# Layer 1's triangular inverses: diagonal blocks of 16 by row steps, joined to 32 by matrix products

## The chip, the cores and the metric

The kernel runs on one core of a Trainium2 chip. The metric is device time in microseconds, the median of three runs. A profiled execution of the kernel before gives the trace from which all times below come. The engines are named as in the profile: PE (matrix products; PEld is its weight load), DVE (vector engine), ACT (activation engine), POOL (GpSimd) and SP (which issues nearly all DMAs).

## The reference, cut to what matters

The reference is one step of a two-layer decoder for 512 prompt tokens and 8 sample tokens, width 1024, float32. Layer 0 mixes windowed attention and a state-space scan; layer 1 is a gated delta net; each is followed by a SwiGLU block. The change touches one thing only, the solve in layer 1's delta rule:

```python
kb = kc * bc[..., None]
a_mat = jnp.einsum('bhcid,bhcjd->bhcij', kb, kc) * dec_strict + jnp.eye(ch)
rhs = jnp.concatenate([vc * bc[..., None], kb * jnp.exp(gcum)[..., None]], axis=-1)
sol = lax.linalg.triangular_solve(a_mat, rhs, left_side=True, lower=True, unit_diagonal=True)
```

For every chunk of tokens and every one of 16 value heads this is a unit lower triangular system, identity plus a strictly lower part made of the keys' products, their decays and beta. The kernel works with chunks of 128 tokens, so it has 4 chunks x 16 heads = 64 systems of 128 x 128, in two groups g of 32 (8 heads by 4 chunks).

## The kernel before, in words

All large projections are float32 products split into hi + lo parts: three products per weight tile, two token halves, 128 output columns at a time (`lin`, line 299, whose products all come from `mm`, line 268). A tile of 128 output columns is 48 PE instructions. The weights are loaded by SP in groups of 1 MB and split by ACT or DVE (hi) and POOL or DVE (lo) in `WStream.split` (lines 148 to 167).

Layer 1 (`l1`, lines 1206 to 1323) goes in this order of the program:

- `kq(g, 0)` (line 1234): four tiles of keys of group g. Each is projected on PE, scaled and convolved (`conv_tile`, line 518: scaling on DVE at line 274, one tap on ACT, one sum on POOL at line 274, multiply-adds on DVE at line 281), and transposed to tokens (`l1_tokens`, PE line 271).
- `l1_system(g)` (line 1423): builds the 32 systems of a group in `s.A[g]` (tiles X and p7): POOL at lines 1439 and 1441 (recorded at the helper's line 274), ACT exponentials, products of keys on PE, a DVE product with them; four 32 x 32 transposes on DVE (line 1457) write the transposed diagonal blocks of 32 to `xt` in p5.
- `l1_eliminate` (line 1461): the inverses of all diagonal blocks of 32, by 31 row steps j for each group, on all 128 partitions at once. A step is two DVE operations: a product of (31 - j) x (j + 1) elements into a scratch in b4 and its subtraction from the rows below in `T` (p5). Both are `tt` (line 274), so the trace shows them as `b<-p` and `p<-p,b`. The steps of the two groups are written alternately. At the end two 32 x 32 transposes per group (lines 1485 and 1486) give the transposed blocks `up` (p5) and the blocks `tn` (b4).
- `l1_combine(g)` (line 1489): blocks of 64 from those of 32, then 128 from 64, by small products on PE into the PSUM ring "ma" (two buffers, `mx`, line 264), with evictions on ACT and DVE between them. A 32-row round is 32 products; two such rounds, twice, and eight rounds of 8 products of 64 rows, for each group.
- `kq(g, 1)` and `l1_queries(g)` (line 1416) for both groups: four tiles of queries each; then a [128, 32] table of query decays is computed on DVE (`sd`), transposed on PE to rows (line 1409, recorded at line 271 as `mb<-cst,sd`), and written to DRAM.
- `v(0)` and `v(1)` (line 1240): eight tiles of values each.
- the two scans (`l1_scan`, line 1547), issued alternately, each chunk's products needing the inverses `U = s.A[g]`, then the sample tokens, the gate projection and the output projection.

Each engine runs its instructions in one fixed order. That order comes from a planner that walks through the program with estimated costs and due times: of the instructions that are ready by its estimate it takes the one that stands first in the program, `high_priority()` work ahead of it. So `l1_eliminate` is preferred to the queries' and values' work wherever its operands are ready. `hold(...)` keeps a stretch of the program from being planned before a given instruction: `hold_v1` is `e030` in the table of choices (line 84), that is, `v(1)` stays behind step 30 of group 0's elimination. `hold_v0` is `s01` (a step of `l1_system(0)`).

What the elimination before consists of:

```python
for j, g in steps:                       # 31 steps, two groups
    nr = 31 - j
    for c0, c1 in ((0, min(j + 1, cut)), (cut, j + 1)):   # cut = 32: one pass
        ...
            s.tt(t, xt[g][:, j, j + 1:32].unsqueeze(2).to_broadcast([128, nr, nn]),
                 T[g][:, j, c0:c1].unsqueeze(1).to_broadcast([128, nr, nn]), ALU.mult, e)
            o = s.tt(T[g][:, j + 1:32, c0:c1], T[g][:, j + 1:32, c0:c1], t, ALU.subtract, e)
```

The scratch of the elimination lies in b4 at 0 and 1024; the combining uses b4 from 0 (`tn`) and from 2048 (the evicted products `zb`); the scans later use b4 for states and decays.

Of the kernel before, what the change touches and what calls it, by code (L numbers as in the profile page):

```python
# [58 lines left out]
def shape_constants():  # L59
# [24 lines left out]
 'hold_v1': 'e030',  # L84
# [37 lines left out]
def KN(n, v, *others):  # L122
    """The engine, share or order chosen at a place: v unless the table has another of the choices."""
    return KNOBS.get(n, v)
# [4 lines left out]
class WStream:  # L129
    """Weights, in the order of use: loaded in groups, split into hi + lo in units of at most 4 row tiles."""  # L130
# [38 lines left out]
    def tile(s, ap, c0, kts, spread=None, ncol=None, out=None):  # L169
        """Yield (row tile, hi, lo) for the 128 columns from c0 and the row tiles kts; input weights come two tiles a load.  # L170
        out = (buffer, offset) of 1024 floats for each four row tiles, to hold them apart from the ring."""
        if ncol is None:
            g = c0 - c0 % 256
            if s.key != (ap.tensor.name, ap.offset, g):
                s.key, s.raw = (ap.tensor.name, ap.offset, g), s.load(ap, 0, 8, g, 256)
            raw, off = s.raw, c0 - g
        else:
            raw, off = s.load(ap, 0, 8, c0, ncol), 0
        for k0 in range(0, len(kts), 4):
            hi, lo = s.split(raw, kts[k0], 4, off, spread, out and out[k0 // 4])  # L180
            for j in range(4):
                yield kts[k0] + j, hi[:, j], lo[:, j]

    def rows(s, ap, c0, loads):
        """As tile() for a tall matrix; loads are (first row tile, count, unit offsets in their order)."""
        for k0, n, offs in loads:
            raw = s.load(ap, k0, n, c0, 128)
            for o in offs:
                m = min(4, n - o)
                hi, lo = s.split(raw, o, m, 0)  # L190
                for j in range(m):
                    yield k0 + o + j, hi[:, j], lo[:, j]


class Ker:
# [14 lines left out]
    def gen(s, *names):  # L210
        """From here on these buffers hold something else: float32r operands and float32 data never share a tile."""
        for n in names:
            s.big[n] = s.sb.tile([128, BIG[n]], F32, tag=n, name=n, bufs=1)

    def lay(s, name, off=0, n=KD, dt=F32R):
        """Operand (tile, half) -> columns, for n tiles of all tokens."""
        t = s.B(name, off, n, NT, dt=dt)
        return lambda k, h: t[:, k, HALF[h]]

    def layh(s, name, n=KD):  # L220
        """As lay(), the first half of the tokens of every tile before the second."""
        return lambda k, h: s.B(name, 256 * n * h + k * HW[h], HW[h], dt=F32R)
# [63 lines left out]
    def cp(s, e, out, in_):  # L286
        """Copy on ACT, DVE or GpSimd."""
# [10 lines left out]
    # ---- linear layers: weights stationary, 520 token columns moving in two halves  # L298
    def lin(s, w, xh, xl, nkt, halves=(0, 1), ps=None):
        """ps[half] = sum over row tiles of w (yielding (row tile, hi, lo)) of hi'xh + hi'xl + lo'xh."""  # L300
# [7 lines left out]
    def group(s, w, xh, xl, nkt):  # L308
        """Up to four tiles, the first half of the tokens of all before the second half, which may come later."""
# [13 lines left out]
    def lnexp(s, ins):  # L323
        """After ins, one table load for Ln and Exp."""
        with s.tc.issue_after(ins):
            s.nc.scalar.preload_act_table_set("natural_log_exp_and_others")

    def rstd(s, out, ps, n, e=EPS, keep=None, after=None):
        """out = rsqrt(ps / n + e), refined by a Newton step; keep = EPS * (ps / n + e)."""
# [17 lines left out]
    # ---- setup  # L347
# [66 lines left out]
    def add_sq(s, h, x, first, tmp, eng=None):  # L414
        """accT += x^2."""
# [7 lines left out]
    def prenorm(s, n, l, hi, lo, h, upd=None):  # L423
        """hi + lo = x * gain, exactly split."""
# [9 lines left out]
    def token_norm(s, h, keep=None):  # L434
        """s.R2 = per-token rsqrt(mean x^2 + eps), on every partition."""
# [7 lines left out]
    def boundary(s, deferred):  # L443
        """x += mp * rsqrt(mean m^2 + eps), then the next layer's prenorm (n, l, hi, lo): the second half, and the norms."""
# [5 lines left out]
    def residual(s, deferred, h):  # L450
        """One half's update of x, as a function of the feature tile."""
# [17 lines left out]
    def out_proj(s, rows, xh, xl, nkt, mp, n, l, pre, tail=2, final=False):  # L469
        """mp = m * gain, accT + sqs = sum m^2 for the eight tiles of an output projection; the last ones by token halves."""  # L470
# [46 lines left out]
    # ---- causal convolution of one 128-feature tile, then silu  # L517
# [26 lines left out]
    def conv_sample(s, nt, new, old, w, bias, out, tmp):  # L544
        """new [128, nt, 8], old [128, nt, 8, 3], w(j) [128, nt]; out [128, nt, 8] = silu(conv)."""
# [12 lines left out]
    def gate_z(s, ps, zt):  # L558
        """zt = silu(z)."""
# [8 lines left out]
    def softplus(s, out, x, n):  # L568
        """out = max(x, 0) + log1p(exp(-|x|)); log1p(e) = 2 atanh(e / (2 + e)) as a series. Shapes [128, n]."""
# [16 lines left out]
    # ---- layer 0: input projection and mixers in the order of issue  # L586
# [78 lines left out]
    # ---- layer 0: sample convolution state  # L665
# [21 lines left out]
    # ---- layer 0: dt, decays in token layout  # L687
# [53 lines left out]
    # ---- layer 0: SSD over four chunks of 128 tokens, for one group of heads  # L741
# [78 lines left out]
    # ---- layer 0: one SSM step per sample  # L820
# [39 lines left out]
    # ---- layer 0: gate, grouped norm  # L860
# [6 lines left out]
    def l0_norm(s, g, zt, yh, yl):  # L867
        """y * silu(z) (in zt), normalised, to the exactly split yh + yl."""
# [11 lines left out]
    # ---- layer 0: attention of the prompt  # L880
# [25 lines left out]
    def l0_tokens(s, hp):  # L906
        """Keys and values token-major: the caches of the prompt and of the samples, V for the products."""
# [82 lines left out]
    # ---- layer 0: attention of the samples over their cached rows  # L990
# [67 lines left out]
    # ---- SwiGLU  # L1058
# [55 lines left out]
    def cache_shift(s):  # L1114
        """The samples' rolling caches: all rows but the oldest move up by one."""
# [11 lines left out]
    def final_early(s):  # L1127
        """x and the norm's eps of the second half token-major."""
# [27 lines left out]
    def final_first(s):  # L1156
        """The first half's outputs; m of the second half token-major, as far as it is known."""
# [26 lines left out]
    def final_last(s):  # L1184
        """The second half's outputs, token-major: x + m * rsqrt(mean m^2 + eps)."""
# [19 lines left out]
    # ---- layer 1: gated delta net, input projection and mixer in the order of issue  # L1205
    def l1(s):
# [64 lines left out]
        for g in range(2):  # L1271
            marks["c%d" % g] = s.l1_combine(g)
# [10 lines left out]
        with hold("hold_v0", "-", "s01", "s02", "s03", "s12", "s13", "e004", "e010", "e020", "e030", "e110"):  # L1283
# [4 lines left out]
        with hold("hold_v1", "e116", "e104", "e110", "e113", "e119", "e122", "e125", "e128", "e130", "c00", "c01", "c02", "c10", "c11", "e020", "e030"):  # L1288
# [36 lines left out]
    def vo(s, g, h, j):  # L1325
        """Half h of the tokens of v head 8 g + j: V token-major, then the outputs feature-major."""
# [5 lines left out]
    # ---- layer 1: beta, decays in token layout  # L1332
# [41 lines left out]
    # ---- layer 1: keys (w = 0) and queries token-major: sums of squares, keys for the state products  # L1374
# [23 lines left out]
    def log_norm(s, g, w):  # L1398
        """-log(sum of squares + eps) / 2 in place, seen per v head."""
# [6 lines left out]
    def bcast_rows(s, t, tag):  # L1406
        """[tokens, 32] to DRAM as 32 rows of 128 tokens."""
# [14 lines left out]
    # ---- layer 1: the 32 (chunk, v head) systems of one half of the heads, I + strictly lower  # L1422
# [37 lines left out]
    # ---- layer 1: transposed unit-triangular inverses in place of the systems: diagonal blocks of 32 by elimination  # L1460
    def l1_eliminate(s, marks):
        nc = s.nc
        cut = KN("cut", 32, 28, 24, 20, 16)
        xt = [s.B("p5", 1024 * g, 32, 32) for g in range(2)]
        T = [s.B("p5", 2048 + 1024 * g, 32, 32) for g in range(2)]
        for g in range(2):
            nc.gpsimd.memset(T[g], 0.0)
            nc.gpsimd.memset(s.B("p5", 2048 + 1024 * g, 1024)[:, 0:1024:33], 1.0)
        steps = [(j, g) for j in range(31) for g in range(2)]
        if KN("eseq", 0, 1):  # L1470
            steps = [(j, g) for g in range(2) for j in range(31)]
        for j, g in steps:
            nr = 31 - j
            for c0, c1 in ((0, min(j + 1, cut)), (cut, j + 1)):
                nn = c1 - c0
                if nn > 0:
                    t = s.B("b4", 1024 * g + 512 * (c0 > 0), nr, nn)
                    e = nc.gpsimd if c0 else None
                    s.tt(t, xt[g][:, j, j + 1:32].unsqueeze(2).to_broadcast([128, nr, nn]),
                         T[g][:, j, c0:c1].unsqueeze(1).to_broadcast([128, nr, nn]), ALU.mult, e)  # L1480
                    o = s.tt(T[g][:, j + 1:32, c0:c1], T[g][:, j + 1:32, c0:c1], t, ALU.subtract, e)
                    if not c0:
                        marks.setdefault("e%d" % g, []).append(o)
# [4 lines left out]
    # ---- layer 1: the inverses of 64 and 128 rows from those of 32  # L1488
# [57 lines left out]
    # ---- layer 1: delta rule over four chunks of 128 tokens, for one half of the heads  # L1546
# [119 lines left out]
    # ---- layer 1: silu(z) times the normalised outputs, split into hi + lo  # L1666
# [16 lines left out]
    # ---- layer 1: sample convolution state  # L1683
# [25 lines left out]
    # ---- layer 1: one delta-rule step per sample: what the states are not needed for  # L1709
# [42 lines left out]
    # ---- layer 1: one delta-rule step per sample: outputs, then (l1_sample_state) states  # L1752
# [133 lines left out]
```

## Time and profile before

| what | us |
|---|---|
| runs | 1904.42, 1915.31, 1905.85 (median 1905.85) |
| span of the profiled execution, first to last instruction | 1901.6 |
| its own time beside the span | not listed; the span is 4.25 below the median of the runs |
| PE busy in the span | 1746.8 |
| DVE busy in the span | 1190.0 |
| first and last elimination operation | 967.62 to about 1104.7 |
| last product of the combining | about 1144.5 |

A row of the trace by time gives its start, its length, the engine, the line, the operation, output and inputs by the program's names, the shape and a count if rows were merged. A float32 product leaves two PE records. PEclk is the clock that PE was granted, 1.0 being full and 0.5 the only lower value in this trace. A wait is put down to the engine that released it.

### The profile page before, as it was taken

The numbers are of one execution on the slowest core, as the hardware profiler recorded it, in microseconds if no ns is written. First come the engines' busy times: TensorE is split into PE (matmuls) and PEld (weight loads), VectorE is DVE, ScalarE is ACT, GpSimd is POOL, SyncE is SP. The second block draws the span as 40 slices with busy tenths as digits, with TensorE's granted clock in tenths as the row PEclk, the third lists the DMA queues.
The fourth block names the chain that finished last, engine by engine and source line by source line (L and its number), as shares of the span: only waits on it lengthen the run. The fifth ranks groups of instructions, "written<-read, shape, count | busy, mean of one in ns | idle before, by whom it ended". The sixth has DMA issues, their size and how long they took to land.

```text
span 1901.6 us, 36269 instructions
## 1 busy us (share of the span) xinstructions
PE 1746.8 (92%) x14263; PEld 1659.2 (87%) x14263; DVE 1190.0 (63%) x2334; ACT 748.7 (39%) x1828; POOL 876.2 (46%) x768
## 2 busy tenths in 40 slices
PE   8899999898999999988968898989889999999996
PEld 7888777698999999977857787978889899999996
DVE  6898878638323221178899977888954954443125
ACT  5432335555222223355756555544334511111222
POOL 2565756234444433435474554646668411112452
PEclk9999999998999999999988899999989899999998
DMA  7345765453333334453442123257998333432333
GB/s 259 125 130 183 237 202 142 145 182 113 111 111 112 112 106 136 124 177 114 137 139 72 59 65 92 63 156 212 272 290 237 132 135 134 134 133 84 92 92 106
DMA packets 293323, 268.88 MB, mean 141 GB/s; under 512 B 11841, under 2 KB 276742, under 8 KB 291986
## 3 DMA queue, kind: packets, MB, share of 16 engines
q1 hardware_dynamic: 292502, 265.90, 45.5%
q8 instruction: 112, 1.84, 0.4%
q10 hardware_dynamic: 652, 0.68, 0.1%
q14 instruction: 57, 0.47, 0.1%
HBM read 241.01 MB, written 62.04 MB: 159 GB/s over the span
## 4 chain that ended last, share of the span: by engine, by line
PE 56%; DVE 26%; DMA 8%; issue 4%; ACT 4%; POOL 2%; SPq 1%; DVEq 0%; POOLq 0%; ACTq 0%
PE acc L268 48%; DVE p L274 4%; DVE cs L281 4%; PE ma L268 4%; PE mb L268 3%; DVE b L274 2%; DVE sq L281 2%; DMA raw<-in_w_ffn_down_dram 2%; DVE p L281 1%; DVE Hh L281 1%; PE mb L271 1%; DVE cs L274 1%; DMA bm<-csd 1%; POOL cs L274 1%; DVE wlo L165 1%
## 5 line engine op out<-in xcount | busy, mean ns | idle before, releaser
L165 POOL TENSOR_TENSOR wlo<-raw,whi 128x512 fp32r<-128x512 f32 (+3 forms) x373 | 500.8, 1346 | 676.7 <-ACT whi L289 368.1
L268 PE MATMUL acc<-Hl,whi 128*128 128x256 f32 (+1 forms) x2576 | 565.6, 291 | 20.2 <-DVE Hl L281 8.5
L268 PEld LDWEIGHTS acc<-Hl,whi 128*128 128x128 f32 x2576 | 420.5, 193 | 35.4 <-issue 11.3
L289 ACT CAST whi<-raw 128x512 fp32r<-128x512 f32 (+3 forms) x392 | 234.4, 602 | 453.0 <-PE acc L268 388.2
L268 PE MATMUL acc<-Hh,whi 128*128 128x256 f32 (+1 forms) x1824 | 387.0, 287 | 3.5 <-DVE cs L274 2.0
L268 PE MATMUL acc<-Hh,wlo 128*128 128x256 f32 (+1 forms) x1824 | 389.0, 288 | 0.0
L268 PEld LDWEIGHTS acc<-Hh,whi 128*128 128x128 f32 x1824 | 292.5, 191 | 8.2 <-issue 5.1
L268 PEld LDWEIGHTS acc<-Hh,wlo 128*128 128x128 f32 x1824 | 292.8, 191 | 7.5 <-issue 6.7
L268 PE MATMUL acc<-bm,whi 128*128 128x256 f32 (+1 forms) x1136 | 237.1, 290 | 1.4 <-DVE bm L281 1.4
L268 PE MATMUL acc<-p,whi 128*128 128x264 f32 (+1 forms) x1280 | 230.6, 287 | 4.4 <-ACT p L1819 1.6
L290 DVE CAST whi<-raw 128x512 fp32r<-128x512 f32 x131 | 61.1, 467 | 256.7 <-PE acc L268 195.2
L165 DVE TENSOR_TENSOR wlo<-raw,whi 128x512 fp32r<-128x512 f32 (+1 forms) x150 | 117.5, 785 | 142.2 <-ACT whi L289 138.8
L268 PEld LDWEIGHTS acc<-p,whi 128*128 128x128 f32 x1280 | 190.6, 192 | 6.4 <-ACT p L1819 1.9
L268 PEld LDWEIGHTS acc<-bm,whi 128*128 128x128 f32 x1136 | 182.1, 193 | 3.7 <-issue 1.6
L268 PE MATMUL acc<-p,wlo 128*128 128x256 f32 (+1 forms) x704 | 164.4, 288 | 8.7 <-DVE wlo L165 7.0
L268 PE MATMUL acc<-Hl,wlo 128*128 128x256 f32 (+1 forms) x752 | 171.1, 293 | 1.0 <-POOL wlo L165 0.9
L268 PEld LDWEIGHTS acc<-Hl,wlo 128*128 128x128 f32 x752 | 126.4, 195 | 3.2 <-POOL wlo L165 1.6
L268 PEld LDWEIGHTS acc<-p,wlo 128*128 128x128 f32 x704 | 119.6, 192 | 10.1 <-DVE wlo L165 7.9
L281 DVE SCALAR_TENSOR_TENSOR cs<-cs,cw 128x512 f32<-128x512 f32 x100 | 96.4, 966 | 12.7 <-POOL cs L274 8.6
L268 PE MATMUL acc<-X,whi 128*128 128x264 f32 (+1 forms) x512 | 100.4, 291 | 1.7 <-DVE X L274 1.3
L268 PEld LDWEIGHTS acc<-X,whi 128*128 128x128 f32 x512 | 80.4, 195 | 3.2 <-DVE X L274 1.6
L281 DVE SCALAR_TENSOR_TENSOR Hh<-cs,CS,Hh 128x256 f32<-128x256 f32 x64 | 53.1, 894 | 26.5 <-POOL Hh L274 26.2
(465 smaller groups left out, 2932.6 us busy)
## 6 DMA issues: line engine op xcount, KB each, us to landing
raw<-in_w_gdn_in_dram SPq DMA_DIRECT2D x24, 1024.0 KB
raw<-in_w_ffn_gate_dram SPq DMA_DIRECT2D x22, 1024.0 KB
raw<-in_w_ffn_up_dram SPq DMA_DIRECT2D x22, 1024.0 KB
raw<-in_w_ffn_down_dram SPq DMA_DIRECT2D x20, 1024.0 KB
raw<-in_w_hyb_in_dram SPq DMA_DIRECT2D x16, 1024.0 KB
out_sv_dram<-in_cache_attn_v_dram SPq DMA_DIRECT2D x16, 1023.0 KB
out_sk_dram<-in_cache_attn_k_dram SPq DMA_DIRECT2D x16, 1023.0 KB
raw<-in_w_gdn_out_dram SPq DMA_DIRECT2D x10, 1024.0 KB
```

The lines of the kernel that those rows point to most:

```text
L165: eng.tensor_tensor(out=lo[:, :nk, d:d + n], in0=raw[:, :, o:o + n], in1=hi[:, :nk, d:d + n].bitcast(F32), op=ALU.subtract)
L268: s.nc.tensor.matmul(out, lhsT=lhsT, rhs=rhs, start=start, stop=stop, skip_group_check=skip)
L271: s.nc.tensor.transpose(out, in_, s.ident[0:in_.shape[0], 0:in_.shape[0]])
L274: return (eng or s.nc.vector).tensor_tensor(out=out, in0=a, in1=b, op=op).ins
L281: return s.nc.vector.scalar_tensor_tensor(out=out, in0=a, scalar=sc, in1=b, op0=op0, op1=op1).ins
L289: return s.nc.scalar.copy(out, in_).ins
L290: return (s.nc.vector if e == "V" else s.nc.gpsimd).tensor_copy(out, in_).ins
```

## The change

The elimination stops at blocks of 16: 15 steps instead of 31. A step now works on both blocks of 16 of each block of 32 in one operation (a first dimension of 2 with the stride from one diagonal block to the next), so that a step is still two DVE operations. A new function `l1_join(g)` makes the blocks of 32 from those of 16: three rounds of 128 products on PE, each of one block (32 systems y, 4 blocks b of 32 rows), 16 columns wide, with one eviction on ACT and two on DVE, and a clearing of half of a scratch `z` on POOL. It is called ahead of `l1_combine(g)`. The table of choices has `hold_v1` at `e014`, the last step of group 0.

```diff
-        steps = [(j, g) for j in range(31) for g in range(2)]
...
-        for j, g in steps:
-            nr = 31 - j
-            for c0, c1 in ((0, min(j + 1, cut)), (cut, j + 1)):
...
+        def both(t, r, c, dims):
+            t = dap(t)
+            return bass.AP(t.tensor, t.offset + 32 * r + c, [list(t.ap[0]), [16 * 33, 2]] + dims)
...
+        for j in range(15):
+            for g in range(2):
+                nr, nn = 15 - j, j + 1
+                t = s.B("b4", 1024 * g, 2, nr, nn)
+                s.tt(t, both(xt[g], j, j + 1, [[1, nr], [0, nn]]), both(T[g], j, 0, [[0, nr], [1, nn]]), ALU.mult)
+                o = both(T[g], j + 1, 0, [[32, nr], [1, nn]])
+                marks.setdefault("e%d" % g, []).append(s.tt(o, o, t, ALU.subtract))
...
+    def l1_join(s, g):
+        nc = s.nc
+        up, tn, A = s.B("p5", 1024 * g, 32, 32), s.B("b4", 1024 * g, 32, 32), s.A[g]
+        z = s.B("b4", 2048, 32, 32)
+        nc.gpsimd.memset(z[:, :, 0:16], 0.0)
+        blocks = [(y, 32 * b) for y in range(32) for b in range(4)]
+        v = lambda ps: ps.rearrange("p (y c) -> p y c", y=32)
+        ps = s.mx("ma")
+        for y, b in blocks:
+            s.mm(ps[b:b + 32, y * 16:y * 16 + 16], A[b:b + 32, y, b:b + 32], up[b:b + 32, y, 16:32])
+        nc.scalar.copy(z[:, :, 16:32], v(ps))
+        pu = s.mx("ma")
+        for y, b in blocks:
+            s.mm(pu[b:b + 32, y * 16:y * 16 + 16], tn[b:b + 16, y], z[b:b + 16, y, 16:32])
+        s.tt(up[:, :, 16:32], up[:, :, 16:32], v(pu), ALU.subtract)
+        pt = s.mx("ma")
+        for y, b in blocks:
+            s.mm(pt[b:b + 32, y * 16:y * 16 + 16], z[b:b + 16, y], tn[b:b + 16, y, 0:16])
+        s.tt(tn[:, :, 0:16], tn[:, :, 0:16], v(pt), ALU.subtract)
...
         for g in range(2):
+            s.l1_join(g)
             marks["c%d" % g] = s.l1_combine(g)
...
- 'hold_v1': 'e030',
+ 'hold_v1': 'e014',
```

The transposes at the end of the elimination, the building of the systems, the combining, the queries, the values and the scans are as before.

More of the change, by code (lines that the diff above doesn't have):

```diff
@@ L1282, in l1 @@
         s.lo_pool = KN("lp_v0", 1, 2, 3, 0)
-        with hold("hold_v0", "-", "s01", "s02", "s03", "s12", "s13", "e004", "e010", "e020", "e030", "e110"):
+        with hold("hold_v0", "-", "s01", "s02", "s03", "s12", "s13"):
             v(0)
@@ L1287, in l1 @@
         s.lo_pool = KN("lp_v1", 1, 2, 3, 0)
-        with hold("hold_v1", "e116", "e104", "e110", "e113", "e119", "e122", "e125", "e128", "e130", "c00", "c01", "c02", "c10", "c11", "e020", "e030"):
+        with hold("hold_v1", "e114", "e014", "c00", "c01", "c02", "c10", "c11"):
             v(1)
@@ L1462, in l1_eliminate @@
         nc = s.nc
-        cut = KN("cut", 32, 28, 24, 20, 16)
         xt = [s.B("p5", 1024 * g, 32, 32) for g in range(2)]
         T = [s.B("p5", 2048 + 1024 * g, 32, 32) for g in range(2)]
+        dap = lambda d: d if isinstance(d, bass.AP) else d[:]
+        def both(t, r, c, dims):
+            t = dap(t)
+            return bass.AP(t.tensor, t.offset + 32 * r + c, [list(t.ap[0]), [16 * 33, 2]] + dims)
         for g in range(2):
@@ L1468, in l1_eliminate @@
             nc.gpsimd.memset(s.B("p5", 2048 + 1024 * g, 1024)[:, 0:1024:33], 1.0)
-        steps = [(j, g) for j in range(31) for g in range(2)]
-        if KN("eseq", 0, 1):
-            steps = [(j, g) for g in range(2) for j in range(31)]
-        for j, g in steps:
-            nr = 31 - j
-            for c0, c1 in ((0, min(j + 1, cut)), (cut, j + 1)):
[L1475 to L1483, printed above, removed]
+        for j in range(15):
[5 more added lines that the diff above has]
+                marks.setdefault("e%d" % g, []).append(s.tt(o, o, t, ALU.subtract))
         for g in range(2):
```

## The prediction

> **What bounds the kernel now.** I read the page first, then the busy times by stage around the elimination, then PE's waits inside those stages, then the rows of single operations. Over the whole span PE is the engine that counts:
>
> ```profile
> span 1901.6 us, 36269 instructions
> ...
> PE 1746.8 (92%) x14263; PEld 1659.2 (87%) x14263; DVE 1190.0 (63%) x2334; ACT 748.7 (39%) x1828; POOL 876.2 (46%) x768
> ...
> PE   8899999898999999988968898989889999999996
> ...
> DVE  6898878638323221178899977888954954443125
> ...
> PEclk9999999998999999999988899999989899999998
> ```
>
> A slice is 47.5 us. In slices 20 to 23 (951 to 1141 us) DVE is at 7 to 9 tenths, PE falls to 6 to 9 and its clock to 8: there the elimination runs. By stages (keys and first system; the first part of the elimination; its rest and the combining; the scans):
>
> ```profile
> core 0: us, PE busy (x) PEld busy (x) DVE busy (x) ACT busy (x) POOL busy (x), PEclk, DMA share, GB/s
> 864.00:967.00 103.00, 92.85 (x740) 89.88 (x741) 91.49 (x154) 67.15 (x191) 51.53 (x48) 0.98 0.42 134
> 967.00:1011.00 44.00, 25.28 (x195) 24.57 (x195) 43.41 (x61) 24.59 (x88) 27.92 (x20) 0.81 0.27 85
> 1011.00:1160.00 149.00, 128.23 (x1520) 122.35 (x1518) 130.21 (x220) 85.79 (x206) 78.89 (x81) 0.91 0.23 69
> 1160.00:1250.00 90.00, 87.72 (x665) 81.61 (x666) 73.57 (x189) 55.23 (x193) 44.19 (x45) 1.00 0.31 82
> ```
>
> From 967 to 1011 DVE is busy 43.41 of 44 us and PE 25.28: DVE is the bound. From 1011 to 1160 both are near full: DVE 130.21 of 149, PE 128.23. PE is idle there for 149 - 128.23 = 20.8 us, nearly all of it explained by waits for DVE:
>
> ```profile
> engine line waited for: us in total, times, longest us
> PE mb L271 <- DVE sd L274: 6.6, 1, 6.6
> PE ma L268 <- issue: 3.5, 1, 3.5
> PE ma L268 <- DVE X L278: 3.1, 1, 3.1
> PE mb L271 <- DVE ex L281: 3.0, 3, 2.0
> PE ma L268 <- DVE Hh L274: 1.7, 2, 1.3
> PE acc L268 <- DVE cs L274: 1.6, 2, 0.9
> ```
>
> So what a freer DVE can give PE back from 1011 on is about 20 us of waits, and the half clock that follows such waits: 0.09 x 149 = 13.4 us of full clock not granted, of which part falls into the idle time itself. Against that stands whatever work the change puts on PE in the same stage. This is the whole question.
>
> **The change, part by part.** *Taken from DVE.* The elimination now:
>
> ```profile
> L274 DVE TENSOR_TENSOR b<-p 128x31 f32<-128x31 f32 (+15 forms) x62 | 37.8, 614 | 0.7
> L274 DVE TENSOR_TENSOR p<-p,b 128x31 f32<-128x31 f32 (+15 forms) x62 | 36.3, 594 | 0.8
> ```
>
> 124 operations, 74.1 us busy. Their lengths without and with company, and the medians:
>
> ```profile
> 967.62 0.18 DVE L274 TENSOR_TENSOR b<-p 128x31 f32<-128x31 f32 x1
> 1039.43 0.29 DVE L274 TENSOR_TENSOR b<-p 128x135 f32<-128x135 f32 x1
> 984.13 2.46 DVE L274 TENSOR_TENSOR b<-p 128x175 f32<-128x175 f32 x1
> L274 DVE TENSOR_TENSOR b<-p x62: 177/390/2455, 967.6 to 1104.2; 128x31 f32<-128x31 f32 x4, 128x60 f32<-128x60 f32 x4, 128x87 f32<-128x87 f32 x4, 128x112 f32<-128x112 f32 x4
> L274 DVE TENSOR_TENSOR cs<-acc,R x85: 356/418/543, 36.1 to 1152.6; 128x256 f32<-128x256 f32 x43, 128x264 f32<-128x264 f32 x42
> ```
>
> ```profile
> 984.04 2.35 POOL L274 TENSOR_TENSOR p<-cst,p 128x1024 f32<-128x1024 f32 x1
> ```
>
> An operation on two SBUF operands that starts beside a POOL operation takes its length (2.46 beside POOL's 2.35); one that reads PSUM (`cs<-acc,R`) never exceeds 0.54. The mean, 0.60, stands some 0.22 above the median 0.39. The new elimination is 15 steps x 2 groups x 2 = 60 operations of 2 x (15 - j)(j + 1) = 30 to 128 elements, 91 on average; between the two rows above that is 0.18 + 0.11 x 60 / 104 = 0.24 us. With the same 0.22 for company: 60 x 0.46 = 28 us (bounds: 14.4 without company, 37 if each keeps today's mean). The four DVE operations of the transposes at the end stay. The join adds, for each group, two DVE subtractions of 128x512 that read PSUM, one ACT copy and half a POOL memset of this size:
>
> ```profile
> L274 DVE TENSOR_TENSOR b<-b,ma x2: 673/674/676, 1155.3 to 1156.8; 128x512 f32<-128x512 f32 x2
> ...
> L289 ACT COPY b<-ma 32x512 f32<-32x512 f32 x8 | 4.6, 571 | 0.4 <-PE ma L268 0.3
> ...
> L1467 POOL MEMSET p<- x2: 946/946/947, 863.1 to 864.0; 128x1024 f32 x2
> ```
>
> DVE +4 x 0.67 = 2.7; ACT +1.1 and POOL +0.9 lie beside other work (ACT is busy 85.79 and POOL 78.89 of the 149). DVE is relieved of 74.1 - 28 - 2.7 = 43 us, most of it after 1011, where it leaves DVE some 95 us of work in 149. DVE stops being the bound there.
>
> *Put on PE.* Six rounds of 128 float32 products of 32 (or 16) rows, 32 columns of weights, 16 moving columns: 768 products, 1536 records. The nearest rows:
>
> ```profile
> 1057.67 1.20 PE L268 MATMUL ma<-p,X 32*32 32x32 f32 x64 [3.54 <-issue]
> ...
> 1070.47 1.20 PE L268 MATMUL ma<-b 32*32 32x32 f32 x64
> 1071.60 1.14 PE L268 MATMUL ma<-X 64*64 64x64 f32 x16
> ...
> L268 PE MATMUL ma<-b 32*32 32x32 f32 x256 | 5.5, 192 | 0.0
> ```
>
> A combining round of 32 products, 64 records, takes 1.20 us; less the last record's own 0.19 that is 1.01 / 63 = 16 ns a record, 32 ns a product. At this price a join round takes 128 x 0.032 = 4.1 us and all six 24.6. Bounds: half of it, 12.3, if 16 moving columns cost half of 32; 28.8 if every 64 records cost a whole 1.20. Entering and leaving such blocks (1.13 us from the start of the 64 records to what follows, against 1.01) adds 0.1 to 0.2 each, 1 us for six. Which end? Rows with a single moving column say that fewer columns do not help:
>
> ```profile
> 1893.29 0.20 PE L268 MATMUL mb<-cst,acc 128*8 128x1 f32 x2
> 1893.35 0.19 PE L268 MATMUL mb<-cst,sd 128*8 128x1 f32 x2
> ```
>
> Two records of one column take 0.06 us from start to start of the pairs, 30 ns each: no cheaper than the 16 ns of the 32-column records, which share the array two by two. I take 24.6. The Trainium skill speaks against this change in the same way: "TensorE: Matmul & The Clock Gate", section "Wait — 56ns, not 53.3ns?", states that the start-to-start of products never drops below about 25 ns however few columns move. By that rule halving the columns saves nothing and the sum keeps 24.6; by array time alone it would have 12.3. The 30 ns rows agree with the rule.
>
> *What becomes of the waits.* From 967 to 1011 I change nothing. Its great loss is one wait of PE for the queries' decay table, in PE's fixed order ahead of the projections of the next queries:
>
> ```profile
> PE mb L271 <- DVE sd L274: 16.1, 1, 16.1
> ```
>
> The operations that hold DVE in that time are elimination steps and convolution beside long POOL operations (the 2.46 above); the new steps are shorter by 0.1 us only, each meets the same POOL work, and since they are planned quicker no fewer of them stand ahead of the table. Bounds: nothing, or all 16.1.
>
> From 1011 on, the steps of group 0 beyond 15 are gone at once, and group 1's end near 1050 instead of 1105:
>
> ```profile
> 1000.00:1030.00 30.00, 11.22 (x21) 0.96 0.31 106
> 1030.00:1060.00 30.00, 17.65 (x44) 0.90 0.12 37
> 1060.00:1105.00 45.00, 26.73 (x43) 0.82 0.16 48
> ```
>
> (DVE's busy time on the elimination and its copies alone.) Of the waits listed I take back 6 of the 6.6 for the second table, all of X (3.1), ex (3.0), Hh (1.7) and cs (1.6), and 1 of the 3.5 ahead of the combining, which stays as the wait of the join for the transposes: 16.4 together. Of the clock I take back 7 of the 13.4. The scans can start as soon as PE has room, since the inverses are ready some 40 us earlier; but PE is busy 87.72 of 90 us there, so I take 1. The join has waits of its own: ACT's copy ahead of its second round, DVE's subtraction ahead of the first combining round. While PE waits there, the values' projections queue behind it, and DVE, ACT and POOL wait for those. The planner fills such places with projections, so I put 2 in all. The join's z shares b4 with group 0's combining, so join 1 follows it; with 40 us in hand that costs nothing, and some 14 us (three rounds of 4.1 and three evictions) if the inverses were the last thing the scans wait for. `hold_v1` at `e014` frees the values earlier than the eight tiles of `v(0)` let them start: nothing. No DMA is added.
>
> *Sum:* + 24.6 + 1 (PE work) + 2 (waits of the join) - 16.4 (waits) - 7 (clock) - 1 (scans) = + 3.2 us. The span 1901.6 lies 4.25 below the runs' median; I leave that as it is: 1905.85 + 3.2 = **1909 us**. The elimination shrinks, DVE is relieved of 43 us, and PE, the next bound, takes back in products what it gains in waits.
>
> **The rivals.** *Faster:* the 16.1 us wait goes as well and the products cost the lower bound. Then 1909 - 16.1 - 12.3 = 1881. For it: DVE is full from 967 to 1011, and a shorter chain may let the table through earlier. Against it: the same number of steps in that stretch, and the 30 ns rows. It decides itself by whether PE's idle time from 967 to 1011 falls below 10 us.
>
> *Slower:* PE's queue stands at the join. Each join has three places where PE needs DVE or ACT (the transposes, the copy, the subtraction): six in all, and the two such places in group 0's combining cost 3.5 and 3.1 us. At 3.3 each that is 20 instead of 2, and with gaps of this length the clock is not won back either: 1909 + 18 + 7 = 1934. For it: the order is planned with estimated costs, and DVE's company with POOL is not in the estimate (0.39 against 2.46). Against it: group 1's combining, from 1108 to 1145 with no elimination beside it, shows no such wait in the list above. It decides from about 3 us a wait on.
>
> *Slower by the bank:* if products of different row blocks that write one PSUM bank can't run side by side, a record of the join costs the 30 ns of a lone one: 256 x 0.03 = 7.7 us a round, 46 in all, 1909 + 21.5 = 1930. Against it: the combining rounds do just this with two row blocks and take 16 ns a record. The Trainium skill, "TensorEngine Tiling (Array Packing)", section "Gotcha 1: PSUM Pressure", states that different row tiles cannot use the same bank at the same time; by these rows that doesn't cost two of them anything, and no run here shows four.
>
> **How the numbers follow.** A measurement of this kernel can tell about 1% (19 us) from no change. Forecast (within 19 us of before) 0.66; faster 0.17; slower at the join's waits 0.14; the bank 0.03. The forecast's own range is 1909 - 12.3 to 1909 + 4.2 + 8 (half the join's waits of the slower rival), 1897 to 1921. To leave out no more than 2 in 10, it has to reach to both rivals' places: 1880 to 1932. Faster by over 1%: 0.17; within 1%: 0.66; slower by over 1%: 0.17.
>
> **What would show it right or wrong.** Right: the elimination's operations are 60 and 22 to 34 us; the six rounds take 4 us each; DVE's share from 1011 to the scans falls to under 75% and PE's busy share there rises above 92%; PE's wait of some 16 us for `sd` is still there. A join round under 3 us, or the wait gone, means the faster rival; PE waits of over 3 us ahead of the join's second round or the first combining round mean the slower one. The forecast is wrong as a whole if PE keeps idle time of 20 us from 1011 on although DVE is free: then something other than DVE's load set those waits.

## The result: 1936 us, slower by 1.4%

The kernel after takes 1936.43 us (median of 4 runs, 1931.88 to 1938.93), the kernel before 1907.82 (4 runs, 1904.42 to 1915.31). The ratio is 1.0139 with a 95% interval of 1.0110 to 1.0167: some 27 us slower, where 3 us slower was forecast, and above the range.

The page of the profile after (this execution took 1938.88 us):

```profile
span 1937.0 us, 39287 instructions
...
PE 1768.5 (91%) x15799; PEld 1680.4 (87%) x15799; DVE 1166.7 (60%) x2274; ACT 750.7 (39%) x1830; POOL 873.3 (45%) x770
...
PE   7889998998999999979967898989889899999996
...
DVE  6898877648233321288997366878964864453115
...
PEclk8999999898999999999987898999889999999998
...
q8 instruction: 124, 2.03, 0.5%
```

PE has 21.7 us more of work (1768.5 against 1746.8), DVE 23.3 us less. The span has grown by 35.4, more than the medians, because the profiled execution after (1938.88) is among the slowest of its four. So 14 us more of it are idle time of PE. In slices 20 to 23 of 48 us each DVE now stands at 9, 7, 3 and 6 tenths: it is free where it was full, and PE still shows 6, 7, 8 and 9. By stages, with the columns of the table before (busy time of each engine, granted clock, share of the DMA engines):

```profile
core 0: us, PE busy (x) PEld busy (x) DVE busy (x) ACT busy (x) POOL busy (x), PEclk, DMA share, GB/s
967.00:1011.00 44.00, 26.55 (x198) 25.81 (x197) 43.42 (x64) 22.33 (x80) 26.62 (x21) 0.81 0.21 75
1011.00:1160.00 149.00, 125.60 (x2901) 120.44 (x2901) 87.53 (x135) 75.51 (x177) 64.68 (x70) 0.85 0.19 59
```

From 967 to 1011 nothing has changed, as forecast, and the wait for the table `sd` is there as before:

```profile
PE mb L271 <- DVE sd L274: 15.9, 1, 15.9
```

From 1011 to 1160 DVE is busy for 43 us less (130.21 to 87.53), and PE is idle for 23.4 us where it was idle for 20.8. The elimination itself came out as worked out, 60 operations of 31.4 us in place of 124 of 74.1:

```profile
L274 DVE TENSOR_TENSOR p<-p,b 128x30 f32<-128x30 f32 (+7 forms) x30 | 16.7, 556 | 0.8
L274 DVE TENSOR_TENSOR b<-p 128x30 f32<-128x30 f32 (+7 forms) x30 | 14.7, 489 | 0.6
```

What PE waits for has changed its name. Its waits from 1011 to 1180, total, times, longest:

```profile
engine line waited for: us in total, times, longest us
PE ma L268 <- issue: 21.0, 10, 3.5
PE mb L271 <- DVE ex L281: 4.1, 5, 2.1
PE ma L268 <- DVE p L274: 0.6, 1, 0.6
```

The waits for DVE are down to 5 us. In their place stand 21 us of "issue": PE waits there for nothing that the profile shows, with products of the ring "ma" next in line. PE's own row by time, around the first join, shows where:

```profile
1019.15 0.41 PE L268 MATMUL acc<-bm,whi 128*128 128x256 f32 x2
1019.48 1.99 PE L268 MATMUL ma<-p,X 32*32 32x16 f32 x217
1023.51 0.73 PE L268 MATMUL ma<-p,X 32*32 32x16 f32 x39 [2.04 <-issue]
1024.17 0.80 PE L268 MATMUL acc<-Hl,wlo 128*128 128x256 f32 x2
1024.77 0.64 PE L268 MATMUL acc<-Hl,whi 128*128 128x256 f32 x2
...
1029.54 0.31 PE L268 MATMUL acc<-Hl,wlo 128*128 128x256 f32 x1
1029.78 1.78 PE L268 MATMUL ma<-b 16*32 16x16 f32 x191
1034.13 1.90 PE L268 MATMUL ma<-b 16*32 16x16 f32 x128 [2.58 <-issue]
1038.41 1.90 PE L268 MATMUL ma<-b 16*32 16x16 f32 x128 [2.38 <-issue]
1043.79 0.89 PE L268 MATMUL ma<-b 16*32 16x16 f32 x53 [3.48 <-issue]
```

Three things are to be seen. The gaps lie in the middle of a round (a round has 256 records), not ahead of one, where a wait for a copy or a subtraction would lie. Between gaps the records run faster than forecast, at either clock: 217 in 1.99 us, less the last one's 0.2, is 8 ns each where the granted clock is 1.00 (1019.4 to 1021.4), and 128 in 1.90 us is 13 ns each where it is 0.50 (1034.1 to 1036). The 16 ns of the forecast came from rows at 1.00. And from the second gap on there are 128 records between them: with a weight load for each, 256 instructions. The projections between the rounds (1024.77 to 1029.54, 22 records, 0.64 us for a pair where it was 0.41 ahead of the join) start 0.43 us a pair apart instead of 0.24: the granted clock is 0.50 from 1024.2 to 1029.5, five microseconds after the first gap.

Two records of the page point to what runs out. Before the change the page had this row (kind of queue, packets, MB):

```profile
q8 instruction: 112, 1.84, 0.4%
```

After it has 124 packets and 2.03 MB. The 12 packets more are 16 KB each (0.19 MB / 12), and PE has 1536 products and 1536 weight loads more: 3072 instructions, 256 for each of the 12. A 16 KB block of 256 instructions, and a gap every 256 instructions. During the second join the trace has such a block each 3.5 to 4.0 us (1081.13, 1084.92, 1088.93, 1092.81, 1096.71, 1100.28, 1103.73). The packets' times settle what ends the gaps: each of the ten ends 1.2 to 1.6 us after a block of this queue has landed (at the first gap the block landed at 1022.07 and PE went on at 1023.51, at the second 1032.68 and 1034.13). The Trainium skill, "Perfetto Trace Analysis", section "The 4-stage abstract model", states that instructions are of 64 bytes; 16 KB / 256 is just that.

**Theory A:** PE's instructions reach it in blocks of 256, one per 3.5 us or so. A burst of products so small that it uses a block up in 1.7 us (128 records of 13 ns) waits for the next; a join round of two blocks costs 7 us whatever its products do. **Theory B:** the products are dear in the array or the bank and the loss grows with their work, or it is the waits between PE, ACT and DVE inside the join. **Theory C:** the changes between the join's small products and the projections of 128 rows are what costs, or row blocks that share a PSUM bank. And for the other half of the sum, **theory D:** DVE's elimination was never what set the time from 1011 on.

### The profile page after: what moved, and what is told of

It is laid out like the page before. It is cut to its first block, busy times and chain, and to the rows that moved or that the text cites. A ratio compares the mean times of both kernels' runs of the same rounds, so it can differ in the third digit from the quotient of the medians.

```text
span 1937.0 us, 39287 instructions
## 1 busy us (share of the span) xinstructions
PE 1768.5 (91%) x15799; PEld 1680.4 (87%) x15799; DVE 1166.7 (60%) x2274; ACT 750.7 (39%) x1830; POOL 873.3 (45%) x770
## 3 DMA queue, kind: packets, MB, share of 16 engines
q8 instruction: 124, 2.03, 0.5%
## 4 chain that ended last, share of the span: by engine, by line
PE 55%; DVE 18%; DMA 6%; ACT 4%; issue 3%; POOL 2%; SPq 0%; DVEq 0%; POOLq 0%; ACTq 0%
PE acc L268 46%; PE ma L268 5%; DVE p L274 3%; PE mb L268 3%; DVE cs L281 2%; DMA raw<-in_w_ffn_down_dram 2%; DVE sq L281 1%; POOL cs L274 1%; DVE b L274 1%; DVE p L281 1%; DVE p L1458 1%; PE mb L271 1%; DVE Hh L281 1%; DVE Hh L274 1%; ACT L284 1%
## 5 line engine op out<-in xcount | busy, mean ns | idle before, releaser
L165 POOL TENSOR_TENSOR wlo<-raw,whi 128x512 fp32r<-128x512 f32 (+3 forms) x373 | 495.2, 1331 | 702.5 <-ACT whi L289 378.9
L268 PE MATMUL acc<-Hl,whi 128*128 128x256 f32 (+1 forms) x2576 | 562.6, 292 | 19.3 <-DVE Hl L281 9.0
```

What stands on the lines that cost most here:

```text
L165: eng.tensor_tensor(out=lo[:, :nk, d:d + n], in0=raw[:, :, o:o + n], in1=hi[:, :nk, d:d + n].bitcast(F32), op=ALU.subtract)
L268: s.nc.tensor.matmul(out, lhsT=lhsT, rhs=rhs, start=start, stop=stop, skip_group_check=skip)
```

## The experiments

The kernel before ran beside them, on two chips: 1909.17 (13 runs) beside the first four of the table, 1909.38 (13 runs) beside the others. Ratios are to those. Where times of two changed kernels are subtracted below, 1936 us among them, the difference is good to a few us: the four runs of the kernel after spread over 7.

| kernel | us | ratio, 95% interval |
|---|---|---|
| after without the join | 1901.41 | 0.9958 (0.9943 to 0.9974) |
| each join product twice | 1978.19 | 1.0365 (1.0346 to 1.0384) |
| join of two rounds | 1924.89 | 1.0083 (1.0057 to 1.0109) |
| join spread among projections | 1948.48 | 1.0210 (1.0189 to 1.0230) |
| 64 moving columns | 1929.92 | 1.0124 (1.0091 to 1.0157) |
| join in pieces of 32 products | 1948.99 | 1.0212 (1.0177 to 1.0246) |
| two rounds, in pieces | 1921.76 | 1.0080 (1.0050 to 1.0110) |
| before, one step of 31 | 1905.25 | 0.9983 (0.9967 to 0.9999) |

**The relief alone (no join).** The change without its addition to PE: the short elimination, and the blocks of 32 are left unjoined.

```diff
         for g in range(2):
-            s.l1_join(g)
             marks["c%d" % g] = s.l1_combine(g)
```

> The changed kernel with the call of the join left out: blocks of 16 go unjoined into the combining, so the inverses miss the lower left quarter of each block of 32. It measures what the relief of DVE is worth without its price on PE. Theory A (PE's instructions don't arrive fast enough: 256 of them, 128 records, each 3.8 us): the join costs 6 rounds x 2 blocks x 3.8 = 46 us plus some 5 us of half clock, so the time is 1936 - 51 = 1885 us, about 20 below the kernel before. Rival B (the join's gaps are waits for its evictions on ACT and DVE, and the relief is worth nothing on PE): what falls away is the join, and what is left is the kernel before, 1905 us or more.

Measured 0.9958: 8 us faster (5 to 11 by the interval), not 24. The time, 1901, lies nearer to B's 1905 than to A's 1885. The join so costs 1936 - 1901 = 35 us net, and the relief of DVE is worth a third of the 24.4 us that the prediction took back; the 20 us of it that theory A had carried over into this expectation fall with it. PE's waits and the stage show why; this kernel, from 1011 to 1160:

```profile
PE ma L268 <- ACT b L289: 5.7, 2, 5.4
PE mb L271 <- DVE ex L281: 3.6, 4, 2.2
PE mb L271 <- DVE acc L281: 3.2, 3, 2.0
PE ma L268 <- DVE p L274: 3.1, 1, 3.1
```

```profile
1011.00:1160.00 149.00, 129.71 (x1552) 123.17 (x1551) 112.65 (x163) 91.98 (x233) 79.71 (x82) 0.94 0.26 80
```

DVE is busy for 17.6 us less than before (130.21 to 112.65), and PE is idle for 19.3 us instead of 20.8. It waits now for the combining's copies (ACT `b`, DVE `p`) and for the convolutions (`ex`, `acc`): as it seems, links of the same chains, at which PE has no other work ready.

**Each join product twice.** It tells a price per instruction from one that is paid once a round.

```diff
         for y, b in blocks:
-            s.mm(ps[b:b + 32, y * 16:y * 16 + 16], A[b:b + 32, y, b:b + 32], up[b:b + 32, y, 16:32])
+            for _ in range(2):
+                s.mm(ps[b:b + 32, y * 16:y * 16 + 16], A[b:b + 32, y, b:b + 32], up[b:b + 32, y, 16:32])
...
```

> The changed kernel with each product of the join issued twice in a row with the same operands and output: 3072 PE instructions more, no dependency more, no eviction more. Theory A (supply of instructions, 3.8 us per 256): 12 blocks more, + 46 us, 1982 us, with a gap of 2 to 3 us on PE after every 128 records. Rival B (waits for evictions; the products themselves run at 13 ns a record): + 1536 x 13 ns = + 20 us, 1956 us, gaps only where a round ends.

Measured 1978.19: 41.8 us above the kernel after, for 3072 instructions more. The page of this kernel shows 12 more blocks, and its waits from 1011 to 1240 twice as many gaps:

```profile
q8 instruction: 136, 2.23, 0.5%
```

```profile
PE ma L268 <- issue: 38.5, 21, 2.5
```

41.8 / 12 = 3.5 us a block, 54 ns a product. Between the gaps the products ran at 14 ns a record (128 in 1.95 us, at half clock), some 21 us for the 1536 records more; the rest is gaps, and each of the 21 ends 1.2 to 1.6 us after a block has landed. B's waits between engines are no more in number here, and can't give 42 us.

**Two rounds instead of three.** The middle round makes the transposed blocks again that the last one makes; one DVE transpose gives them too.

```diff
-        pu = s.mx("ma")
-        for y, b in blocks:
-            s.mm(pu[b:b + 32, y * 16:y * 16 + 16], tn[b:b + 16, y], z[b:b + 16, y, 16:32])
-        s.tt(up[:, :, 16:32], up[:, :, 16:32], v(pu), ALU.subtract)
         pt = s.mx("ma")
...
+        nc.vector.transpose(out=s.B("p5", 1024 * g, 1024), in_=s.B("b4", 1024 * g, 1024))
```

> The changed kernel with the middle round of the join and its subtraction taken out; the transposed blocks come instead from one 32 x 32 transpose on DVE of the blocks that the last round mends. 512 products instead of 768, the same result. Theory A: 4 blocks of 256 instructions fall away, 15.4 us, and two transposes of 2 us join the path of a DVE that is free: 1936 - 12 = 1924 us (1919 to 1928). Rival B (waits for evictions): two evictions of 0.7 become two of 2 us, 256 products of 26 ns fall away: 1936 - 7 + 3 = 1932 us.

Measured 1924.89, with 120 blocks on the page and these gaps (960 to 1200):

```profile
PE ma L268 <- issue: 10.5, 4, 4.0
```

Four blocks less, 11.5 us less: 2.9 a block, the same as the 35 us of the whole join by 12. A's forecast of 1924 us is met, B's of 1932 is not. This is a better version than the change, though still 0.8% slower than before.

**64 moving columns.** The same number of products, each with four times the columns.

```diff
-            s.mm(ps[b:b + 32, y * 16:y * 16 + 16], A[b:b + 32, y, b:b + 32], up[b:b + 32, y, 16:32])
+            s.mm(ps[b:b + 32, min(y * 16, 448):min(y * 16, 448) + 64], A[b:b + 32, y, b:b + 32], wide(up)[b:b + 32, y * 30:y * 30 + 64])
...
```

> The changed kernel with 64 moving columns in each product of the join instead of 16: the same 768 products and instructions, four times the array work. The outputs of neighbouring systems overwrite each other, so the joined blocks are not the right ones. Theory A (256 PE instructions arrive each 3.8 us): a block of 128 records that ran in 1.75 us now runs in about 3.9 (60 ns a product), the gaps after it are filled, and the time stays: 1938 us (1932 to 1946). Rival B (the gaps are waits of their own, for evictions or ends of rounds, and the products' running time adds to them): 12 x (3.9 - 1.75) = + 26, 1962 us.

Measured 1929.92, ratio 1.0124 beside the change's 1.0139, and 2 us below A's range: four times the columns cost nothing. The second and third round and the gaps of this kernel, by time and from the list of waits (960 to 1190):

```profile
1027.79 13.99 PE L268 MATMUL ma<-b 16*32 16x64 f32 x510
```

```profile
PE ma L268 <- issue: 4.3, 4, 1.3
```

510 records in 13.8 us without a gap, 27 ns each at a granted clock of 0.50: a block of 128 records in 3.45 us. The array now takes about as long as the next block does to come, and the gaps have filled with work. B falls: neither the array's time nor the bank's sets the 42 us. The granted clock from 1011 to 1160 is 0.89 here, against 0.85 with the gaps.

**The join among the projections, two ways.** If a block takes 3.5 us to come, the join is best written among products that last longer. First two join products after each product of the values' projections:

```diff
                 for h in halves:
                     s.mm(ps[h], lhs, x(kt, h), st, sp)
+                    for _ in range(2):
+                        next(s.fill, None)
...
```

> The changed kernel with the join's products written between the products of the values' projections, two after each, so that a stretch of 256 PE instructions takes as long as its successor needs to arrive; z moves to a buffer of its own (the spent T of its group), so that group 1's join need not follow group 0's combining; the combining of group 0 stands after four tiles of values, that of group 1 after eight. All 768 products stay. Theory A: the 21 us that PE waits for nothing shown inside the join go, with some half clock: 1936 - 21 - 4 = 1911 us (1905 to 1920), and the gaps after every 128 records are gone. Rival C (row blocks sharing a PSUM bank, or the drain at each change between 32-row and 128-row products, are what costs): the changes between the two kinds of product grow from a dozen to hundreds, and the time rises above 1945 us.

Measured 1948.48, worse, as C said. The planner found few projections ready where the first join stands, so most of it still came in bursts, and most of the gaps stayed (960 to 1200):

```profile
PE ma L269 <- issue: 15.6, 7, 6.0
```

Where it did alternate, PE's row by time reads:

```profile
1110.23 0.29 PE L269 MATMUL ma<-b,p 16*32 16x16 f32 x4
1110.45 0.58 PE L269 MATMUL acc<-bm,whi 128*128 128x256 f32 x1
1110.96 0.29 PE L269 MATMUL ma<-b,p 16*32 16x16 f32 x4
1111.18 0.59 PE L269 MATMUL acc<-bm,whi 128*128 128x264 f32 x1
```

A period of four join records and one projection takes 0.73 us. At the granted clock there, 0.50, 4 x 13 ns and half of a pair's 0.43 make 0.27. There is no gap in it, and no shortage of instructions (10 in 0.73 us). What is left is the change to and fro between small and large products; the trace doesn't show what in it takes the 0.46 us. So larger pieces, 32 products after every eight of a projection, which the planner has to keep behind these eight:

```diff
+    def tick(s, ins):
+        s.nt += 1
+        if s.nt % 8 == 0:
+            with s.tc.issue_after(ins):
+                for _ in range(32):
+                    next(s.fill, None)
...
```

> The changed kernel with the join cut into pieces of 32 products, each held behind 8 more products of the values' projections (group 0 from the fourth tile of values on, group 1 from the ninth), z in a buffer of its own. All 768 products stay. Theory A: 32 products and 8 projections, 144 instructions in some 2 us, need about the rate at which instructions arrive, so the gaps of 2 to 3 us go, 21 us to about 5, and 24 changes between 32-row and 128-row products cost 0.2 to 0.5 us each: 1936 - 16 - 4 + 8 = 1924 us (1916 to 1932). Rival C (the changes are the cost): 24 instead of 6 of them and no gain, 1940 us or more.

Measured 1948.99. Here most of the gaps of theory A are gone (list of waits, 960 to 1190), and the time went up all the same; the stage and PE's row by time in the midst of it:

```profile
PE ma L269 <- issue: 3.8, 3, 2.0
...
PE ma L269 <- DVE Hh L282: 3.7, 2, 3.5
```

```profile
1011.00:1160.00 149.00, 137.26 (x2864) 126.95 (x2865) 82.03 (x130) 74.12 (x173) 61.13 (x67) 0.79 0.19 57
```

```profile
1038.27 1.05 PE L269 MATMUL ma<-p,b 16*32 16x16 f32 x64
1039.25 0.80 PE L269 MATMUL acc<-bm,whi 128*128 128x256 f32 x2
1039.85 0.64 PE L269 MATMUL acc<-Hl,wlo 128*128 128x256 f32 x2
1040.28 0.64 PE L269 MATMUL acc<-Hl,whi 128*128 128x256 f32 x2
...
1041.28 1.05 PE L269 MATMUL ma<-p,b 16*32 16x16 f32 x64
```

The granted clock from 1011 to 1160 is 0.79. The eight projections of a period start 0.43 us a pair apart, half speed, and take 2.0 us instead of 1.0; the 32 products take 1.0. So the gaps were saved and half clock was paid: (1 - 0.79) x 149 = 31 us of full clock, against 22 in the kernel after and 13 before. But the clock alone doesn't account for the time: 17 us of gaps saved against 9 of clock would be a gain, and the kernel is 13 us slower than the change. Of the 10 us between the two profiled executions some 6 are lost by the end of the values' projections (the products `ma<-Hh,X` behind them start at 1181.18 instead of 1175.39), the others behind it, where the wait of 3.5 us for DVE `Hh` has come. What sets them was not tested. That A's gaps vanish once other work lies between the blocks agrees with A; A's times of both these expectations were missed. C's times were met, and the half clock between small products is the part of its mechanism that the trace shows.

The two rounds in such pieces:

> The kernel with the middle round replaced by a transpose on DVE, cut into the same pieces: 512 products. Theory A: the 10.5 us that PE still waits for nothing shown with two rounds fall to 3 or less, 16 changes cost 3 to 6 us: 1925 - 8 + 4 = 1921 us (1914 to 1926). Rival C: 1930 us or more. No theory puts it below the kernel before: the join left out altogether gave 0.42% only.

Measured 1921.76, ratio 1.0080, where A put it, but also the same as the 1.0083 of two rounds in bursts. Issue gaps are 3.6 us instead of 10.5 here and the clock is 0.90 in both: with a third less of the join, pieces neither help nor hurt, so A's number is met without the gain that it forecast, and C's (1930 or more) is not.

**Hardly any elimination in the kernel before.** The other half of the sum by itself: 4 DVE operations instead of 124, no join, nothing put on PE.

```diff
-        for j, g in steps:
+        for j, g in steps[:2]:
...
-                        marks.setdefault("e%d" % g, []).append(o)
+                        marks["e%d" % g] = [o] * 31
```

> The kernel before with the first of its 31 elimination steps alone for each group (4 DVE operations instead of 124); blocks of 32, transposes and combining stay, the inverses are wrong. It asks whether the elimination's load on DVE sets PE's waits at all. The prediction's step (it does): the 16 us wait and most of the 20 us later go, and 7 us of clock: 1909 - 40 = about 1870 us. Rival D (the waits belong to the chains that the planner lays end to end, projection, convolution, transpose, eviction, and only move): no more than twice the 8 us that leaving out the join showed, 1893 us or more.

Measured 1905.25, ratio 0.9983 (0.9967 to 0.9999): 3 us from 74 us of DVE work left out. Its waits from 960 to 1190 and its stages:

```profile
PE acc L268 <- DVE cs L274: 9.3, 2, 8.9
PE mb L271 <- DVE p L281: 5.5, 2, 3.2
PE mb L271 <- DVE ex L281: 3.5, 3, 2.1
PE mb L271 <- DVE acc L281: 3.4, 2, 3.0
PE mb L271 <- DVE sd L1411: 1.9, 1, 1.9
PE mb L271 <- DVE sd L274: 1.9, 1, 1.9
```

```profile
967.00:1011.00 44.00, 28.11 (x181) 26.50 (x179) 34.77 (x36) 21.54 (x83) 26.38 (x21) 0.77 0.24 75
1011.00:1160.00 149.00, 134.58 (x1578) 128.54 (x1579) 103.39 (x134) 93.07 (x227) 81.05 (x85) 0.93 0.26 80
```

The wait of 16 us for the table `sd` is gone (two of 1.9 are left), and one of 8.9 us for the scaling of a convolution has come; from 967 to 1011 PE has 15.9 us idle where it had 18.7. From 1011 on it is idle for 14.4 instead of 20.8. D's time is met (1893 or more) and the prediction's step is not (about 1870): DVE's load by the elimination is worth 3 us. That the waits are those of a chain (projection, scaling, convolution, transpose), as D has it, fits their new names but was not tested by itself, since the planner lays the whole order anew for each kernel.

## Why the prediction was wrong

**The step that failed first is the price of the join's products**, "128 x 0.032 = 4.1 us and all six 24.6". The price was read from combining rounds of 64 records, 128 instructions. Such a round uses only half a block of 256, so its row can't show what a longer burst costs. The rounds of the join cost 41.8 us by doubling and 35 net by leaving them out, against 27.6 forecast with their entries and waits. The products' own execution was dearer in the forecast than in the trace: at full clock a record takes 8 ns, so that 1536 would take 12.7 us, close to the lower bound that the prediction named and did not take; with the half clock behind the gaps they run for some 18. The gaps, 21 us, are what the sum did not have. Whether the 8 ns instead of 16 come from 16 columns or from four row blocks was not separated; with 64 columns, records in four blocks take 14 at full clock (217 in 3.25 us). The one "issue" wait that the prediction had, "[3.54 <-issue]", was no such gap: it stands ahead of a round, and the last block had landed 5.9 us before it ended.

**The second, and the larger, is what was taken back**: 16.4 us of waits, 7 of clock and 1 of the scans, 24.4 in all. The join left out, the relief gave 8 us; nearly the whole elimination left out, 3. Some 16 us of the miss lie here, and 7 in the join. The list of waits names who came last, not what the time would be without it: with DVE relieved and no join, 19.3 of PE's 20.8 us of idle time in this stage stayed, under other names. The prediction had named this sign ("wrong as a whole if PE keeps idle time of 20 us from 1011 on although DVE is free"), and it came: 23.4 us.

**The third is the clock.** Instead of 7 us gained, the share from 1011 to 1160 fell from 0.91 to 0.85, some 9 us of full clock; in the kernel without the join it rose to 0.94. Projections run at half speed for some microseconds behind the first gap of each join, and between the small products of the kernel in pieces. This loss is contained in the 42 and the 8 us measured, not a term beside them. The Trainium skill, "TensorE: Matmul & The Clock Gate", section "What's actually happening", states that an idle window of about 3.4 us drops PE to half its clock and a busy one of that length restores it. The five microseconds at half speed after 1024 are of that order, yet here they follow a gap of 2.04 us, and in the kernel in pieces the granted clock is 0.50 from 1108.7 to 1132.6 with PE busy from 1109.7 on.

The sum with the terms as measured: 35 net for the join, less 8 of relief, is 27; the difference measured is 27 to 29. The 35 follow from the same runs and so are no test of the sum, but the rows of the kernel after bear them out: the join's records run for some 18 us and the gaps take 21, in part where PE would have waited anyway, since the 19 us of other waits in the kernel without the join are down to 2.5 (1011 to 1160). Why the doubled products cost 42 was not settled.

**Right were** the elimination (forecast 28 us, measured 31.4), the wait for `sd` that stays (16.1, then 15.9), the rivals' mechanisms that did not come (the wait stays; PE waits 0.6 us only at the join's places for DVE), and that four row blocks in one bank cost nothing that shows. On this last the Trainium skill, "TensorEngine Tiling (Array Packing)", section "Gotcha 1: PSUM Pressure", says that different row tiles can't use one bank at a time. Here four of them writing one bank took 8 ns a record, less than the 16 of two at the same clock. DVE's relief of 43 us matches the stage's 43 in part by chance: the kernel is behind there, so that less of its other work falls into the stage (ACT and POOL are busy 10 and 14 us less too), and over the whole span DVE is busy 23.3 us less. The slower rivals' times, 1930 and 1934, came close to the measured one by mechanisms that the trace rules out.

The rule of the Trainium skill quoted in the prediction ("TensorE: Matmul & The Clock Gate", section "Wait — 56ns, not 53.3ns?"), the floor of about 25 ns a product, was used there for a ratio only. Its figure taken for each of the 1536 records gives an estimate of 38 us, near the 42. But the trace has bursts at 8 and 13 ns, so these products don't keep the floor, and the agreement is in the mean, not in the cause.

What stays open: that small products between projections hold PE's clock at half was seen, and why was not settled; what an alternating period spends 0.46 us on is not known; a join with products of 128 rows on block-diagonal operands, a quarter as many, was not tried. No version here beats the kernel before: the best join (two rounds) is at 1.008, and with a relief worth 8 us, any join has to cost PE less than that.

## What to carry to other kernels

Price a long run of small products by their number of instructions as well as by the rate of a short run: here 256 instructions came per 3.5 us, 54 ns for a float32 product of four, however few columns it moved. Before work is moved off an engine because another waits for it, ask what that engine waits for next; a kernel that leaves the work out answers it for the price of one run, and here it said 3 us for 74. An "issue" wait inside a run of tiny products, ending just after a packet of the instruction queue has landed, is the sign that instructions, not data, are late.

## What the runs showed of the hardware

- Small products of 16 columns in four row blocks run at 8 ns a record at a granted clock of 1.00 and at 13 ns at 0.50, until the instructions run out; those of 32 columns in two row blocks took 16 ns at 1.00.
- Instructions come in blocks of 16 KB, 256 each: 112, 120, 124 and 136 packets for 0, 2048, 3072 and 6144 more PE instructions, to the block. Every "issue" gap of these stretches ended 1.2 to 1.6 us after a block had landed (10 gaps, and 21 with the products doubled).
- Alternating four 16-row records with one 128-row projection took 0.73 us a period, where their own times at that clock (0.50) make 0.27, with no gap in the trace.
- The granted clock is lower with small products between large ones, in pieces even while PE is busy (0.50 from 1108.7 to 1132.6): 0.94 without the join, 0.85 with it in bursts, 0.79 in pieces (with two rounds 0.90 in both).
